# Two-layer trunk on one core: layer B's q as seven half-size block products, with a changed start and an fp32r broadcast

## The chip, the cores and the metric

The kernel runs on one core of a Trainium2 chip. The metric is the device time of one execution in microseconds. TensorE multiplies, VectorE and ScalarE work on the results in PSUM and SBUF, GpSimd (POOL) does a few element operations, SyncE (SP) and ScalarE issue the DMAs.

## The reference

Two layers over x of 1024 tokens by 1024 channels, batch 1, in fp32:

```python
# layer A (gMLP)
u, v, z = split(rms_norm(x) @ w_in)              # 1024 -> 3 x 2048
v = layer_norm(gelu(v))                          # then mixed along 128-token chunks, causal, 8 groups
h = x + rms_norm((gelu(u) * (w_s @ v + b_s) * silu(z)) @ w_out)
# shared keys and values
k, v = rms_norm(h) @ w_k, rms_norm(h) @ w_v      # 4 kv heads of 64
# layer B (sliding window of 128, attention sinks, ALiBi)
q, z = split(rms_norm(h) @ b_w_in)               # 16 heads of 64, and a gate of 1024
o = softmax(q k' / 8 + alibi, with a sink) @ v   # blocks of 128 tokens see the block before and their own
out = h + rms_norm((o * silu(z)) @ b_w_out)
```

## The kernel before, in words

Every product in fp32 is made of three fp32r matmuls: each operand is split into a high part (rounded to fp32r by a ScalarE copy) and a low part (the rest, a VectorE subtraction); mm3 (L168 to 171) adds hi x hi, hi x lo and lo x hi into one PSUM bank. A step of work on TensorE therefore needs splits on ScalarE and VectorE: split (L104 to 106), and split_scaled with a gain (L108 to 110).

The tokens are treated in two halves of 512 (half 0 and half 1), the channels in k-tiles of 128. Activations lie transposed, channels on partitions and 512 tokens on the free axis; a pair of tiles (pair) holds the high and low parts of all 8 k-tiles of one half.

The stages, in the order in which TensorE runs them, with the times of the profile:

- v, and then u and z of layer A, up to 490 us. These large products use a scheme of block products: the operands are cut in two along tokens, inner and outer dimension, and seven products of half-size blocks, of sums of blocks, replace eight. T[1] to T[7] are the seven sums of blocks on the activation side. uz_layer runs them in groups of four products (quads) with weight sums from POOL and VectorE. The row factors 1/rms of x are laid across the partitions in broadcast_rstd (L272 to 279): a diagonal matrix per half, multiplied by a matrix of ones in fp32 (L278), under the v products.
- The output product of layer A (out_layer), 490 to 654 us, in seven products too. Its tail, chain_a (L746 to 758), adds the residual for one half, stores h1, and takes the row factor r1 of the result. norm_h1 (L760 to 773) then multiplies by r1 (hb), transposes it on TensorE (nt), and splits it into n, the operand of layer B: n0 for half 0, n1 for half 1. For half 0 all this is done inside out_layer.
- Layer B in plain products. q of half 0 (654 to 701 us) runs with chain_a for half 1 as a side job, one side step per step of the main one. kv of half 0 (701 to 725 us) runs with norm_h1 of half 1 at its side, and z of half 0 (725 to 769 us) by itself.
- attn(0) (769 to 886 us) and attn(1) (894 to 1005 us): for each block of 128 tokens and half of the heads a unit of scores (s), masks and row maxima on VectorE, exponentials on ScalarE, transposes (pt), and products with v (o). TensorE alone would idle between them, so attn takes steps from a fill, a generator of other products: 64 steps in attn(0), which are kv, q and half of z for half 1; in attn(1) the rest of z and the first output products. The last output products end the kernel.

The weights of layer B come through the class Weights (L112 to 152): a written list, order, of transfers of 512 KB that are loaded into three raw buffers (wload) two places ahead and split one place ahead, in the order in which the products ask for them. Before, the list is q, kv and z for half 0, kv, q and z for half 1, then the output weights. A weight of q is so loaded and split twice, once for each half.

q_phase (L966 to 976) evacuates each of q's PSUM banks at once: a ScalarE copy with the head's scale (L971) for the high part, and a VectorE operation (L972) for the low part, both on 64 partitions for each parity of heads. kv_phase (L989 to 1020) ends with eight ScalarE copies of k (L1017, L1018), subtractions for k's low part (L1019) and copies of v. Unit (scores at L1050, exponentials at L1065) reads q, and kh and kl, the parts of k.

At the start (L403 to 427) SyncE's queue begins with x's first tile, and ScalarE's queue with the gains and then the first half of the first v weights. POOL makes the high part of those weights (L415), VectorE the low part (L418).

Rows of an engine stand in program order, and each engine takes its own rows in that order.

## Time and profile before

| | before |
|---|---|
| median of 3 runs | 1050.68 us (1050.01 to 1051.42) |
| the profiled execution | 1051.56 us |
| its span | 1049.8 us |
| mean granted TensorE clock | 0.998 |
| TensorE, busy share of the span | 99% |
| VectorE | 70% |
| ScalarE | 55% |
| POOL | 19% |

The profile is of one execution. Busy means that an instruction ran on the engine; matmuls overlap one another, so the rate of matmuls is read from the distance between the starts of two. A wait names the engine and line that waited, and the engine and line that ended the wait. In the chain of waits each piece of work is followed back to what released it. The windows of the trace give busy time and number of instructions for each engine in a stretch. In a row of groups the columns are: line, engine, operation, output and inputs with shapes, count, total us and mean ns, and the idle time ahead of them.

### The profile page before, as it was taken

The page shows a single profiled execution, that of the slowest core. Times are in us where ns is not written, and L with a number is a line of the kernel's source. Part 1 is how long each engine was busy: PE and PEld are TensorE (multiplying, and loading weights), DVE is VectorE, ACT ScalarE, POOL GpSimd, SP SyncE. Part 2 cuts the span into 40 slices and gives each one's busy share as a digit, 9 for nine tenths or more (in the row PEclk, how much of TensorE's full clock was granted, in tenths as well). Part 3 has the DMA queues.
Part 4 walks back from the last instruction along what each step waited for, and adds up shares of the span by engine and source line. Part 5 has one row for each costly group of instructions (what it writes and reads, how often), then busy time and mean ns, then how long its engine had stood idle before and what let it go on. Part 6 is the DMA issues. An engine that isn't in the chain of part 4 may idle for free.

```text
span 1049.8 us, 13661 instructions
## 1 busy us (share of the span) xinstructions
PE 1039.2 (99%) x4994; PEld 854.8 (81%) x4994; DVE 731.9 (70%) x1244; ACT 577.2 (55%) x989; POOL 195.2 (19%) x153
## 2 busy tenths in 40 slices
PE   9999999999999999999999999999999999999997
PEld 7888788888888888888888888888888777877776
DVE  6997466867768668677697587665247776667763
ACT  6683444555465565555444464654466665786631
POOL 0300003253342542530200000100001111011120
PEclk9999999999999999999999999999999999999999
DMA  8877252334333333347897642532222121211363
GB/s 310 271 282 269 101 177 88 116 105 143 124 121 116 132 124 117 108 137 272 322 352 270 201 160 93 200 102 86 95 81 71 51 81 61 81 61 61 121 220 120
DMA packets 80899, 157.56 MB, mean 150 GB/s; under 512 B 5824, under 2 KB 32704, under 8 KB 80832
## 3 DMA queue, kind: packets, MB, share of 16 engines
q1 hardware_dynamic: 76176, 147.75, 41.2%
q10 hardware_dynamic: 4656, 8.94, 2.4%
q8 instruction: 39, 0.64, 0.3%
q14 instruction: 28, 0.23, 0.1%
HBM read 125.21 MB, written 31.46 MB: 149 GB/s over the span
## 4 chain that ended last, share of the span: by engine, by line
PE 93%; DVE 4%; ACT 1%; issue 0%; DMA 0%; POOL 0%; DVEq 0%; POOLq 0%; ACTq 0%
PE ob L169 6%; PE ub L169 6%; PE ub L171 6%; PE ob L171 6%; PE ob L170 6%; PE ub L170 6%; PE qz L169 5%; PE qz L171 5%; PE qz L170 5%; PE uc L169 3%; PE uc L171 3%; PE uc L170 3%; PE s L1050 3%; PE sp L614 3%; PE vb L170 2%; PE vb L171 2%
## 5 line engine op out<-in xcount | busy, mean ns | idle before, releaser
L110 DVE SCALAR_TENSOR_TENSOR wlo<-raw_w,gn,whi 128x512 fp32r<-128x512 f32 x80 | 58.7, 758 | 62.2 <-ACT whi L109 62.0
L169 PE MATMUL qz<-n_hi,whi 128*128 128x512 f32 x256 | 101.0, 394 | 0.4 <-DVE q_lo L972 0.4
L171 PE MATMUL qz<-n_hi,wlo 128*128 128x512 f32 x256 | 100.0, 391 | 1.2 <-DVE wlo L110 1.2
L170 PE MATMUL qz<-n_lo,whi 128*128 128x512 f32 x256 | 99.8, 390 | 0.0
L109 ACT ACTIVATE whi<-raw_w,gn 128x512 fp32r<-128x512 f32 x80 | 54.9, 716 | 54.2 <-PE qz L170 35.0
L1065 ACT ACTIVATE pr<-pr,mx 128x129 f32<-128x129 f32 x128 | 50.0, 393 | 40.1 <-DVE mx L1061 40.0
L169 PEld LDWEIGHTS qz<-n_hi,whi 128*128 128x128 f32 x256 | 48.0, 188 | 16.6 <-issue 6.5
L105 ACT ACTIVATE uzhilo_g<-f 128x1024 fp32r<-128x1024 f32 x31 | 32.9, 1060 | 48.6 <-PE uc L171 42.7
L171 PEld LDWEIGHTS qz<-n_hi,wlo 128*128 128x128 f32 x256 | 48.0, 188 | 12.3 <-DVE wlo L110 2.1
L170 PEld LDWEIGHTS qz<-n_lo,whi 128*128 128x128 f32 x256 | 48.1, 188 | 9.3
L106 DVE TENSOR_TENSOR uzhilo_g<-f,uzhilo_g 128x1024 fp32r<-128x1024 f32 x31 | 39.0, 1257 | 19.9 <-ACT uzhilo_g L105 19.9
L209 ACT ACTIVATE uz_slots<-ub 128x512 f32<-128x512 f32 x48 | 28.3, 590 | 42.4 <-PE ub L171 39.0
L169 PE MATMUL ub<-T,whi_g 128*128 128x512 f32 x128 | 50.7, 396 | 0.0
L169 PE MATMUL ub<-T,uzhilo_g 128*128 128x512 f32 x128 | 50.5, 395 | 0.0
L171 PE MATMUL ub<-T,wlo_g 128*128 128x512 f32 x128 | 49.9, 390 | 0.0
L171 PE MATMUL ub<-T,uzhilo_g 128*128 128x512 f32 x128 | 49.9, 390 | 0.0
L170 PE MATMUL ub<-T,uzhilo_g 128*128 128x512 f32 x128 | 49.8, 389 | 0.0
L170 PE MATMUL ub<-T,whi_g 128*128 128x512 f32 x128 | 49.8, 389 | 0.0
L169 PE MATMUL uc<-T,uzhilo_g 128*128 128x512 f32 x124 | 48.9, 395 | 0.0
L170 PE MATMUL uc<-T,uzhilo_g 128*128 128x512 f32 x124 | 48.3, 389 | 0.0
L171 PE MATMUL uc<-T,uzhilo_g 128*128 128x512 f32 x124 | 48.3, 389 | 0.0
L105 ACT ACTIVATE whi_g<-raw_uz 128x1024 fp32r<-128x1024 f32 (+1 forms) x31 | 26.5, 854 | 36.7 <-PE ub L170 15.6
(332 smaller groups left out, 3071.4 us busy)
## 6 DMA issues: line engine op xcount, KB each, us to landing
raw_uz<-in_wuz_in_dram SPq DMA_DIRECT2D x32, 512.0 KB, 3.4
raw_w<-in_wqz_dram SPq DMA_DIRECT2D x32, 512.0 KB, 3.5
td<-uz_slots SPq DMA_DIRECT2D x56, 256.0 KB, 2.2
orawP2a<-td SPq DMA_DIRECT2D x28, 512.0 KB, 4.0
raw<-in_wv_in_dram SPq DMA_DIRECT2D x17, 512.0 KB, 4.8
vg<-vd SPq DMA_DIRECT2D x8, 1024.0 KB, 5.4
orawP2b<-in_wo_a_dram SPq DMA_DIRECT2D x16, 512.0 KB, 7.7
vraw<-in_wv_in_dram SPq DMA_DIRECT2D x13, 512.0 KB, 4.4
```

The source lines that it names most:

```text
L105: nc.scalar.activation(hi, src, AF.Copy)
L106: nc.vector.tensor_tensor(lo, src, hi.bitcast(F32), ALU.subtract)
L109: nc.scalar.activation(hi, src, AF.Copy, scale=g)
L110: nc.vector.scalar_tensor_tensor(lo, src, g, hi.bitcast(F32), ALU.mult, ALU.subtract)
L169: nc.tensor.matmul(out, lhsT=a_hi, rhs=b_hi, start=start, stop=False, skip_group_check=True)
L170: nc.tensor.matmul(out, lhsT=a_hi, rhs=b_lo, start=False, stop=False, skip_group_check=True)
L171: nc.tensor.matmul(out, lhsT=a_lo, rhs=b_hi, start=False, stop=stop, skip_group_check=True)
L209: nc.scalar.activation(out, a, AF.Copy)
L614: nc.tensor.matmul(psv[:, n], lhsT=d["vg"][:, 4 * j + n, i * P:(i + 1) * P], rhs=d["wc"], start=True, stop=True)
L1050: nc.tensor.matmul(pss[par][:, g, w0:256], lhsT=q[par][:, m, bs_], rhs=w[par][:, p, ks], start=g + k == 0, stop=g + k == 2, skip_group_che ...
L1065: nc.scalar.activation(pr[:, i], pr[:, i], AF.Exp, bias=mx[:, i:i + 1], scale=-1.0, accum_out=dn[:, i:i + 1])
```

## The change

Layer B's q, for both halves at once, becomes a stage of its own with seven block products. z of half 0 is put ahead of it, since the block sums need both halves' norms.

- norm_sums replaces norm_h1 for half 1: beside n1 it forms T[1] to T[7]. For each of the four token blocks VectorE makes three differences from the transposed bank (nt1) and splits of T5, T6 and T4, and POOL four additions; a last step splits T7. It runs as side job to z of half 0, after chain_a.
- q_tiles runs four quads of weights, each with seven products of 12 matmuls; its sums of weights are on POOL, its gains and splits on VectorE and ScalarE, its banks are copied or added into six slots and stored to DRAM (qd). The weights of q are loaded once.
- z of half 0 is stored to DRAM (zd) as it is made, and loaded back before attn(0), since its tiles serve as pieces for q_tiles.
- reload_q brings q back from qd, a transfer of 512 KB for each of four steps per half, and makes q's high and low parts with two ScalarE and two VectorE operations of 64 x 1024. Two steps for half 0 run under kv of half 0; the other two and the four of half 1 are a side job of attn(0).
- The tiles of attention (bp) are allocated, and their constants loaded, after q_tiles, not before. kv of half 0 follows q_tiles. attn(0) has a fill of 32 steps in place of 64, four of them taken ahead of the first scores.
- The list of weights is z, kv, kv, z, output weights, and stops after the first eight until q_tiles ends.
- broadcast_rstd multiplies in fp32r: the diagonal is split into two parts, four matmuls in all.
- At the start the first half of the first v weights leads SyncE's queue, and x's first tile goes to ScalarE's, behind the gains.

TensorE has 48 rows fewer. On VectorE, right behind the row factor of half 1 (r_1), the order in before is (yoa is h1 of half 1 by token block, wlo the low part of a weight, qz a bank of q, hb the normalised rows):

```order
L178 TENSOR_SCALAR r_1_90<-s_1_4999 128x4
L763 TENSOR_SCALAR hb_2_5318<-yoa_3_4273,r_1_90 128x1024
L110 SCALAR_TENSOR_TENSOR wlo_5097<-raw_w_5024,gn,whi_5096 128x4x128 x2
L972 SCALAR_TENSOR_TENSOR q_hi<-qz_0_0_4959,qsc,q_hi 64x512
L763 TENSOR_SCALAR hb_3_5352<-yoa_3_4273,r_1_90 128x1024
L972 SCALAR_TENSOR_TENSOR q_hi<-qz_0_1_4960,qsc,q_hi 64x512
L972 SCALAR_TENSOR_TENSOR q_lo<-qz_0_0_4959,qsc,q_lo 64x512
```

and in after (nt_2 is the transposed bank, t_2, qT and q_slots hold block sums):

```order
L180 TENSOR_SCALAR r_1_90<-s_1_5002 128x4
L786 TENSOR_SCALAR hb_2_5071<-yoa_3_4285,r_1_90 128x1024
L110 SCALAR_TENSOR_TENSOR wlo_5135<-raw_w_5027,gn,whi_5134 128x4x128 x2
L786 TENSOR_SCALAR hb_3_5149<-yoa_3_4285,r_1_90 128x1024
L106 TENSOR_TENSOR n_lo<-nt_2_0_5089,n_hi 128x4x128
L208 TENSOR_TENSOR t_2_5087<-nt_2_0_5089,n_hi 128x512
L106 TENSOR_TENSOR n_lo<-nt_2_1_5104,n_hi 128x4x128
L208 TENSOR_TENSOR q_slots<-nt_2_1_5104,n_hi 128x4x128
L208 TENSOR_TENSOR t_2_5088<-nt_2_1_5104,t_2_5087 128x512
```

The evacuations of q are gone from this place, and the sums and splits of the block operands stand there.

In attn(0), VectorE's order between the first units' scores in before (s are the scores, pr and mx probabilities and maxima, snk the sinks):

```order
L110 SCALAR_TENSOR_TENSOR wlo_5934<-raw_w_5805,gn,whi_5933 128x512
L1055 COPY_PREDICATED s_0_10_5911<-mrg,neg 128x2x128
L110 SCALAR_TENSOR_TENSOR wlo_5934<-raw_w_5805,gn,whi_5933 128x512
L1061 ISA pr_0_5839,mx_0_5840<-s_0_10_5911,bias,snk 128x128
L1061 ISA mx_0_5840 128x1
```

and in after (raw_q is the buffer of a reload):

```order
L1221 ISA pr_0_6199,mx_0_6200<-s_0_10_6255,bias,snk 128x128
L1221 ISA mx_0_6200 128x1
L1132 SCALAR_TENSOR_TENSOR q_hi<-raw_q_2_6249,qsc,q_hi 64x1024
L1132 SCALAR_TENSOR_TENSOR q_lo<-raw_q_2_6249,qsc,q_lo 64x1024
L1215 COPY_PREDICATED s_0_11_6256<-mrg,neg 128x2x128
L1221 ISA pr_0_6199,mx_0_6200<-s_0_11_6256,bias,snk 128x128
```

A weight's low half stood ahead of the scores s_0_10 and behind their mask; now a reload's two operations stand between s_0_10 and s_0_11.

The diff, cut to its core (what is left out is allocation and the code of functions named above that changes names only):

```diff
-            q, z = ([(wqz[i, m:m + 4, :, kq * 256:kq * 256 + 256].rearrange("m p c -> p m c"), f"q{kq}")
-                     for m in range(0, 8, 4) for kq in range(4)] for i in range(2))
+            z = [(wqz[1, m:m + 4, :, kq * 256:kq * 256 + 256].rearrange("m p c -> p m c"), f"q{kq}")
+                 for m in range(0, 8, 4) for kq in range(4)]
             kv = [(wkv[kp], f"kv{kp}") for kp in range(4)]
-            self.order += q + kv + z + kv + q + z
+            self.order += z + kv + kv + z
...
+            self.limit = 8
         def load(self, i):
-            while len(self.raw) <= min(i, len(self.order) - 1):
+            while len(self.raw) <= min(i, self.limit - 1):
...
+    def broadcast_rstd(pool):
+        ones_r = pool.tile([P, P], F32R, name="ones_r")
+        copy(ones_r, ones)
         for h in range(NH):
-            dg = sum_tile(f"dg{h}")[:, 0:512].rearrange("p (a b) -> p a b", a=4)
+            dg = st.tile([P, 2, 4, P], F32R, tag="xt", name=f"dg{h}")
             for j in range(4):
-                nc.vector.tensor_scalar(dg[:, j], ident, rx[h][:, j:j + 1], None, ALU.mult)
+                r = rx[h][:, j:j + 1]
+                nc.scalar.activation(dg[:, 0, j], ident, AF.Copy, scale=r)
+                nc.vector.scalar_tensor_tensor(dg[:, 1, j], ident, r, dg[:, 0, j].bitcast(F32),
+                                               ALU.mult, ALU.subtract)
             ps = bank("s", f"bc{h}")
-            nc.tensor.matmul(ps, lhsT=ones, rhs=dg.rearrange("p a b -> p (a b)"), start=True, stop=True)
+            for i in range(2):
+                nc.tensor.matmul(ps, lhsT=ones_r, rhs=dg[:, i].rearrange("p a b -> p (a b)"),
+                                 start=i == 0, stop=i == 1)
...
-        xload(xa[:, 0], 0, 0, 0, 1)
         r0 = raws.take("v0")
-        nc.scalar.dma_start(out=r0[:, 0:512], in_=wv_in[0, 0][:, 0:512])
+        load(r0[:, 0:512], wv_in[0, 0][:, 0:512])
+        xload(xa[:, 0], 0, 0, 0, 1, nc.scalar)
...
+        for t in (2, 3, 0, 1):
+            ts_ = slice(t * P, (t + 1) * P)
+            xt = st.tile([P, D], F32, tag="xt", name=f"hb1_{t}")
+            nc.vector.tensor_scalar(xt, yo[t], r1[1][:, t:t + 1], None, ALU.mult)
+            yield
+            t1, t2 = tmp("t1", t), tmp("t2", t)
...
+                split(n[0][:, ks, ts_], n[1][:, ks, ts_], ps)
+                if kq == 0:
+                    add(t1, ps, n_0[0][0][:, :, ts_].bitcast(F32), ALU.subtract)
+                    add(t1, t1, n_0[1][0][:, :, ts_].bitcast(F32), ALU.subtract, nc.gpsimd)
+                else:
+                    add(t3[:, :, ts_], ps, n[0][:, 0:HT, ts_].bitcast(F32), ALU.subtract)
+                    add(t2, ps, t1, ALU.subtract)
+                    add(t4, n_0[0][1][:, :, ts_].bitcast(F32), t2, ALU.subtract, nc.gpsimd)
+                    add(t3[:, :, ts_], t3[:, :, ts_], n[1][:, 0:HT, ts_].bitcast(F32), ALU.subtract, nc.gpsimd)
+                    add(t4, t4, n_0[1][1][:, :, ts_].bitcast(F32), ALU.add, nc.gpsimd)
+                yield
+            for m, src in ((6, t2), (5, t1)):
+                split(T[m][0][:, :, ts_], T[m][1][:, :, ts_], src)
+            yield
+            split(T[4][0][:, :, ts_], T[4][1][:, :, ts_], t4)
+            yield
+        T[7] = tuple(big.tile([P, HT, TH], F32R, tag=f"P1_{2 + i}", name=f"qT7_{i}") for i in range(2))
+        for i in range(2):
+            split(*(a[:, 2 * i:2 * i + 2] for a in T[7]), t3[:, 2 * i:2 * i + 2])
...
+        def product(q, m, ps, first):
+            hi, lo = ops[q][m]
+            for k in range(HT):
+                cs = slice(k * P, (k + 1) * P)
+                mm3(ps, hi[:, cs], lo[:, cs], T[m][0][:, k], T[m][1][:, k], first and k == 0, k == HT - 1)
...
+        def store(q, i, j, c):
+            nc.sync.dma_start(out=qd[j][q][:, i], in_=c)
...
+        for q in range(5):
+            live = q < 4
+            if live:
+                b = bank("mm", f"qb{q}")
+                product(q, 1, b, True)
+                c00 = slot()
+                copy(c00, b)
+            else:
+                weights.limit = len(weights.order)
+                weights.load(weights.at + 1)
+            if q > 0:
+                pb, pcc, c01 = prev
+                product(q - 1, 4, pb, False)
+                c10 = slot()
+                copy(c10, pb)
+                store(q - 1, 1, 0, c10)
+            if live:
+                a = bank("s", f"qa{q}")
+                product(q, 2, a, True)
+                add(c00, c00, a, ALU.add)
+                store(q, 0, 0, c00)
+                prep1(q + 1)
+            else:
+                weights.split(weights.at)
+            if q > 0:
+                product(q - 1, 3, pcc, False)
+                add(c01, c01, pcc, ALU.add)
+                store(q - 1, 0, 1, c01)
+                del ops[q - 1]
+            if not live:
+                break
+            prep3(q)
+            product(q, 6, b, False)
+            c01 = slot()
+            copy(c01, b)
+            cc = bank("mm", f"qc{q}")
+            product(q, 5, cc, True)
+            prep2(q + 1)
+            fetch(q + 2)
+            product(q, 7, b, False)
+            c11 = slot()
+            copy(c11, b)
+            add(c11, c11, cc, ALU.add)
+            store(q, 1, 1, c11)
+            prev = (b, cc, c01)
...
+    def reload_q(h, q):
+        for i in range(4):
+            r = raw_tile(f"q{h}_{i}").rearrange("p (m t) -> p m t", m=2)
+            nc.sync.dma_start(out=r, in_=qd[h][i])
+            ms = slice(2 * i, 2 * i + 2)
             for par in range(2):
                 rw, ot = half[par], half[1 - par]
-                g = qsc[rw, m // 4:m // 4 + 1]
-                nc.scalar.activation(q[par][rw, m], ps[rw], AF.Copy, scale=g)
-                nc.vector.scalar_tensor_tensor(q[par][ot, m], ps[rw], g, q[par][rw, m].bitcast(F32),
+                g = qsc[rw, i // 2:i // 2 + 1]
+                nc.scalar.activation(q[par][rw, ms], r[rw], AF.Copy, scale=g)
+                nc.vector.scalar_tensor_tensor(q[par][ot, ms], r[rw], g, q[par][rw, ms].bitcast(F32),
                                                ALU.mult, ALU.subtract)
-        for m in range(0, 8, 4):
-            yield from qz_four(h, 0, m, n, evac)
-    def z_phase(h, n, z, m0, m1):
+            yield
...
+                if keep:
+                    nc.sync.dma_start(out=zd[m // 2], in_=zs)
...
+    def attn(h, q, z, fill, total, late=0, first=0, side=iter(())):
         taken = [0, 0]
+        for _ in range(first):
+            step(fill)
...
+            step(side)
...
+    side = chain(chain_a(1, yo, ss), norm_sums(n1, yo, n0))
+    z0 = [qp.tile([P, 4, TH], F32, tag=f"half{i}", name=f"z0_{i}") for i in range(2)]
+    main = z_phase(0, n0, z0, 0, 8, keep=True)
+    qs = q_tiles()
     step(main, main)
-    for _ in main:
+    for i, _ in enumerate(main):
         step(side)
+        if i in (22, 27):
+            step(qs)
...
+    drain(qs)
+    qp_ctx.close()
...
+    side = chain(reload_q(0, q0))
+    z0 = [big.tile([P, 4, TH], F32, tag=f"P1_{2 * i}", name=f"z0_{i}") for i in range(2)]
+    for i, _ in enumerate(kv_phase(0, n0)):
+        if i in (1, 6):
+            step(side)
+    for i in range(4):
+        nc.sync.dma_start(out=z0[i // 2][:, i % 2 * 2:i % 2 * 2 + 2], in_=zd[i])
+    z1 = [big.tile([P, 4, TH], F32, tag=f"P1_{2 * i}", name=f"z1_{i}") for i in range(2)]
     q1 = pair("P3", "q1")
-    fill = chain(kv_phase(1, n1), q_phase(1, n1, q1), z_phase(1, n1, z1, 0, 4))
-    attn(0, q0, z0, fill, 64)
+    fill = chain(kv_phase(1, n1), z_phase(1, n1, z1, 0, 4))
+    attn(0, q0, z0, fill, 32, first=4, side=chain(side, reload_q(1, q1)))
```

More of the change, by code (lines that the diff above doesn't have):

```diff
@@ L984, in evac @@
                 nc.scalar.activation(zs, zs, AF.Silu)
+                if keep:
+                    nc.sync.dma_start(out=zd[m // 2], in_=zs)
         for m in range(m0, m1, 4):
[L987 removed]
+            yield from z_four(h, m, n, evac)
     def kv_phase(h, n):
[L990 to L991 removed]
+        pk = [bank("mm" if h else "s", f"pk{h}_{i}") for i in range(2)]
+        pv = [bank("mm" if h else "s", f"pv{h}_{i}") for i in range(2)]
         for kp in range(4):
@@ L1104, in values @@
             split(q[0][:, ms, bs_], q[1][:, ms, bs_], yt)
-    def attn(h, q, z, fill, total, late=0):
+    def attn(h, q, z, fill, total, late=0, first=0, side=iter(())):
         taken = [0, 0]
+        for _ in range(first):
+            step(fill)
         n = 34 if late else 40
@@ L1218, in tile_yoco @@
-    drain(side)
-    drain(z_phase(0, n0, z0, 0, 8))
+    drain(qs)
+    qp_ctx.close()
+    bp = ctx.enter_context(tc.tile_pool(name="bp", bufs=1))
+    bias = bp.tile([P, 4, P], F32, name="bias")
+    nc.sync.dma_start(out=bias.rearrange("p a b -> p (a b)"), in_=consts[:, C_BIAS:C_BIAS + 512])
+    mrg = bp.tile([P, P], F32, name="mrg")
+    nc.sync.dma_start(out=mrg, in_=consts[:, C_MERGE:C_MERGE + P])
+    neg = bp.tile([P, 1], F32, name="neg")
+    nc.vector.memset(neg, -1e30)
+    kh = [bp.tile([P, 2, S], F32R, name=f"kh{i}") for i in range(2)]
```

131 lines of the change are left out of this document (94 added, 37 removed).

## The prediction

> **What bounds the kernel now.** I read the page first, then TensorE's waits, then the rates of single instructions, and last the busy times by stage. The page's span and its chain by engine:
>
> ```profile
> span 1049.8 us, 13661 instructions
> ...
> PE 93%; DVE 4%; ACT 1%; issue 0%; DMA 0%; POOL 0%; DVEq 0%; POOLq 0%; ACTq 0%
> ```
>
> TensorE carries the chain. Everything it waited for, outside the last stage's idle end (columns: engine and line, what it waited for, us in total, times, longest):
>
> ```profile
> PE qz L171 <- DVE wlo L110: 1.2, 2, 0.7
> PE warm L924 <- DVE small L93: 1.1, 1, 1.1
> PE vb L169 <- POOL whi_v L415: 0.5, 1, 0.5
> PE qz L169 <- DVE q_lo L972: 0.4, 1, 0.4
> PE vb L169 <- ACT ve L209: 0.3, 1, 0.3
> PE vb L170 <- DVE wlo_v L418: 0.2, 1, 0.2
> ```
>
> Under 4 us in all: a matmul less is time less, as long as nothing else comes late. So the question is what the removed matmuls uncover. The profiled execution took 1051.56 us, 1.8 more than its span and 0.88 above the median of the runs, 1050.68. I sum changes against 1051.56 and take 0.88 off at the end. About 0.2% (2.1 us) is what a measurement of this kernel can tell from no change.
>
> **Matmuls removed.** Two neighbours in the timeline (start, duration), and the old broadcast in the chain (start, length):
>
> ```profile
> 655.00 0.39 PE L170 MATMUL qz<-n_lo,whi 128*128 128x512 f32 x1
> 655.68 0.39 PE L170 MATMUL qz<-n_lo,whi 128*128 128x512 f32 x1
> 106.08 1.72 PE bc L278 x4
> ```
>
> Three matmuls start in 0.68 us: 0.227 each, though each is listed with 0.39. Layer B's q took 8 products by 8 k-tiles by 3 matmuls for each half, 384; now 4 quads x 7 products x 12 = 336. 48 x 0.227 = **-10.9**. The broadcast becomes four fp32r matmuls at 0.23: 1.72 - 0.9 = **-0.8**. Its diagonals move to ScalarE and VectorE under the v matmuls, and TensorE had no wait there.
>
> **Start.** The first matmuls wait for weights, not for x:
>
> ```profile
> 5.78 1.24 POOL L415 CAST whi_v<-raw_v 128x512 fp32r<-128x512 f32 x2 [5.28 <-DMA raw_v<-in_wv_in_dram]
> 6.45 0.98 PE L169 MATMUL vb<-whi_v,T 128*128 128x512 f32 x3 [0.51 <-POOL whi_v L415]
> 7.63 0.51 PE L170 MATMUL vb<-wlo_v,T 128*128 128x512 f32 x1 [0.20 <-DVE wlo_v L418]
> ```
>
> The weight transfer moves from second on ScalarE's queue to first on SyncE's. The idle times in the brackets, 0.5 and 0.2, are the most there is to win; x comes later in turn, so I take **-0.3** (-1 to +0.5).
>
> **Waits of before that go.** The two qz rows of the waits sit in q(0), where weight splits and q's evacuations shared VectorE: 1.2 + 0.4 = **-1.6** (if the splits still come late, -0.4). The four together: -13.6.
>
> **Stage z(0): T operands must be made.** The new order runs z(0) first, and under it all seven block operands are built from both halves' norms. Half 1's norm needs r1:
>
> ```profile
> 654.10 0.39 PE L169 MATMUL qz<-n_hi,whi 128*128 128x512 f32 x1
> 672.36 1.01 POOL L179 TENSOR_TENSOR r<-r,small 128x4 f32<-128x4 f32 x1 [12.68 <-DVE r L178]
> 673.40 0.76 DVE L763 TENSOR_SCALAR hb<-yoa,r 128x1024 f32<-128x1024 f32 x1 [1.12 <-POOL r L179]
> 674.07 1.41 DVE L110 SCALAR_TENSOR_TENSOR wlo<-raw_w,gn,whi 128x512 fp32r<-128x512 f32 x2
> 707.60 1.28 DVE L106 TENSOR_TENSOR n_lo<-nt,n_hi 128x512 fp32r<-128x512 f32 x2
> 23.35 1.22 DVE L206 TENSOR_TENSOR sch<-vraw,raw 128x1024 f32<-128x1024 f32 x1
> 702.41 0.87 PE nt L769 x8
> ```
>
> After r1 before's VectorE had four hb, eight n_lo splits, weight halves and q's evacuations to do, spread over q(0) and kv(0), 71 us; now all of it, with 24 more sums and splits for the operands, stands in one queue under z(0)'s 48 us (both queues' beginnings stand in the section on the change). Counted from TensorE's first matmul of the stage (654.1): r1 is there at 673.4, 19.3 us in. Behind it VectorE does hb 4 x 0.75 = 3.0, weight halves 8 x 0.705 = 5.6, 20 operations on a PSUM bank at 0.64 = 12.8, 12 between SBUF tiles at 0.6 (half of the 1.22 row) = 7.2, the two halves of T7 2.4, the first scaled q weight 1.2 and its split 1.2: 33.4, so q's first low half is ready at 52.7. TensorE has 192 matmuls of z and 4 of q at 0.227 (44.5) and four groups of transposes at 0.87 (3.5): it is there at 48.0. **+4.7**. Bounds: 2.3 if only the wait for hb_2 shows (TensorE reaches its transposes 17.7 us in, after 78 matmuls, and hb_2 is there at 20.0), 11 if ScalarE's high halves and POOL's 16 additions put one third of that queue's 20 us of sums on top.
>
> The four quads behind it I cost at nothing: per quad VectorE has two scalings and three splits of 1.2, one half split and three additions of 0.64, 8.6 us under 84 x 0.227 = 19.1 us of matmuls. Should that cover go, each 1 us too late in a quad costs 4. The stores of q and z are not waited for until the reloads, a stage later.
>
> **Entry of attn(0).** The first scores need half 0's k, and only one step pair of kv(1) stands between them and kv(0)'s last matmul, where before all of z(0) did:
>
> ```profile
> L1017 ACT ACTIVATE kh<-pk 64x512 fp32r<-64x512 f32 x4 | 2.4, 593 | 2.2 <-PE pk L171 2.2
> 704.50 0.28 PE L169 MATMUL pv<-whi,n_hi 128*128 128x256 f32 x1
> 704.62 0.28 PE L170 MATMUL pv<-wlo,n_hi 128*128 128x256 f32 x1
> ```
>
> Six ScalarE copies at 0.59 and one subtraction at 0.64 are 4.2; the pair covers 6 x 0.227 + 12 x 0.12 = 2.8: **+1.4** (0 to 3).
>
> **attn(0).** Its fill loses 16 steps of q for the reloads. The stage, and three stretches with busier engines (columns: window, length; then busy us and instructions of TensorE, its weight loads, VectorE, ScalarE, POOL; clock, DMA share, GB/s):
>
> ```profile
> 769.00:886.40 117.40, 116.95 (x646) 92.85 (x644) 87.83 (x250) 76.34 (x208) 15.29 (x14) 1.00 0.20 64
> 20.00:50.00 30.00, 30.00 (x133) 24.49 (x132) 29.99 (x31) 17.32 (x22) 8.22 (x2) 1.00 0.78 264
> 826.00:851.00 25.00, 24.55 (x128) 18.93 (x127) 21.14 (x62) 17.15 (x50) 3.28 (x3) 1.00 0.20 64
> 800.00:890.00 90.00, 89.56 (x450) 67.76 (x449) 68.04 (x184) 56.63 (x152) 14.19 (x13) 1.00 0.20 65
> ```
>
> TensorE had 116.95. Between the first scores and the last values stand 254 qz matmuls in before and 127 of z in after, 24 of pv and 12 of pk less: 116.95 - 127 x 0.227 - 24 x 0.12 - 12 x 0.227 = 82.5. What moved out is paid elsewhere and in the 48. VectorE's rows:
>
> ```profile
> L110 DVE SCALAR_TENSOR_TENSOR wlo<-raw_w,gn,whi 128x512 fp32r<-128x512 f32 x33 | 24.6, 772 | 13.9 <-ACT whi L109 13.9
> L972 DVE SCALAR_TENSOR_TENSOR q_lo<-qz,qsc,q_lo 64x512 fp32r<-64x512 f32 x8 | 6.0, 755 | 1.2 <-ACT q_lo L971 1.0
> 659.71 2.48 DVE L753 SCALAR_TENSOR_TENSOR yoa<-yoa,rpa,xa 128x1024 f32<-128x1024 f32 x2 [1.19 <-POOL rpa L179]
> ```
>
> From 87.83 go 16 evacuations (two groups of 8 like the q_lo row, 12.0) and 16 weight halves (11.3 at 0.705); 12 reload operations of 1,024 columns at 1.24 come (14.9): 79.4. TensorE and VectorE now need almost the same time, so VectorE's own gaps decide. The stretch from 20 to 50 us says what happens where nothing else binds it (30.0 of 30 busy, TensorE without a gap: stall 0), that from 826 to 851 runs at 0.85 (79.4 / 0.85 = 93.4, stall 10.9). In attn(0) itself VectorE's gaps were
>
> ```profile
> DVE dn L1070 <- ACT pr L1065: 4.4, 5, 0.9
> DVE z L1103 <- PE o L1099: 1.7, 1, 1.7
> DVE q_lo L106 <- ACT q_hi L105: 1.4, 2, 0.7
> ```
>
> waits inside a unit's own chain of scores, exponentials and values, which stay: 7.5 of the 90 us window. At a density of 1 - 7.5/90 = 0.917 the stage takes 86.6, **+4.1** over TensorE's 82.5 (0 to 10.9). The others of its waits were for weights or transposes that stood behind q's matmuls and go with them.
>
> **Sum**: -13.6 + 4.7 + 1.4 + 4.1 = **-3.4**: 1048.2 for the profiled execution, **1047.3** as a median. The matmuls' gain is real, and three quarters of it is handed back to VectorE. With the bounds of the three stalls, 2.3 to 11, 0 to 3 and 0 to 10.9, its own range is about 1040 to 1053; all three at one end at once is unlikely, so 1042.5 to 1052.
>
> **Rivals.**
>
> **A, slower: the reloads stop VectorE's queue.** Six reload steps lie in attn(0), each a transfer of 512 KB, then ScalarE's high half and VectorE's low half. VectorE takes its instructions in order, and in after the reload's two stand between one unit's scores, so their lateness delays what TensorE waits for:
>
> ```profile
> raw_w<-in_wqz_dram SPq DMA_DIRECT2D x32, 512.0 KB, 3.5
> ```
>
> A transfer of this size lands 3.5 us after its issue, and ScalarE's copy of 1,024 columns adds some 1.1 (twice the kh row's 0.59, less the fixed part): 4.6 us from a free buffer to VectorE's turn. If a quarter of that is uncovered at each step, 1.15 x 6 = 6.9 come on top of the forecast: **1054.2**. It decides from 3.4 / 6 = 0.6 us lost at each step. For it: the two operations stand ahead of the same unit's next scores. Against it: three raw buffers let a transfer start early, and the DMA engines are only 0.20 busy in the stage.
>
> **B, all but the norm hidden.** VectorE is as dense as at 20 to 50 us, and the entry's copies are done beneath kv(1): -13.6 + 4.7 = -8.9, **1041.8**. For it: the dense stretch, and the idle VectorE of the waits was mostly slack. Against it: units depend on ScalarE at each step.
>
> **C, no change: POOL and VectorE hold each other up.** In the first layer POOL's addition of two tiles next to a busy VectorE ran longer than undisturbed ones:
>
> ```profile
> L206 POOL TENSOR_TENSOR f<-raw_uz,f 128x512 f32<-128x512 f32 x15 | 22.4, 1495 | 0.0
> L206 POOL TENSOR_TENSOR f<-raw_uz,raw_uz 128x512 f32<-128x512 f32 x15 | 19.2, 1281 | 127.2 <-DVE uzhilo_g L106 127.2
> ```
>
> 0.2 us each. If VectorE loses that at each of the 16 additions that POOL does in z(0), its queue there is 3.4 longer and TensorE waits for all of it: -3.4 + 3.4 = 0.0, **1050.7**. The Trainium skill states this as a rule ("SBUF — State Buffer", section "Who interferes with whom"): a VectorE operation with both inputs in SBUF and a GpSimd operation that reads SBUF share a port pair, and the one that comes second is blocked for the whole of the other. An estimate by that rule alone, with a whole 1.28 us lost at each of the 16, would be 20.5 us more. The 0.2 of the trace bears out that there is a cost, and not one of that size.
>
> That the change doesn't do what it says is excluded by the order: 48 rows less on TensorE.
>
> **How the numbers follow.** The forecast 0.43, B 0.22, A 0.22, C 0.13. B and most of the forecast's own range (0.33 of 0.43) are faster by over 0.2%, 0.55; C and 0.08 of the forecast lie within 0.2%, with 0.02 of C's on the slow side, 0.19; A, that and 0.02 of the forecast are slower, 0.26. The range reaches down past B to 1040.5 (B with the bound of 2.3 in z(0) would be 1039.4), and up past A to 1056.5 (a third of the 4.6 uncovered at each step: 1.53 x 6 = 9.2); I leave about 0.1 out on either side.
>
> **What would show it.** In the profile of after: TensorE waits at the first transposes and at qb for a low half, 4 to 5 us in the z(0) and q stages together; s of the first unit waits 1 to 2 us for kl or kh; between the first s and the last o of half 0 the stage is near 86.6 us with VectorE over 0.9 busy. Waits of q_hi or q_lo on the reload's ScalarE copy or on its transfer, over 0.6 us each, would speak for A; a stage of 83 us for B; POOL additions over 1.4 us in z(0) with TensorE waiting longer there for C. The forecast is wrong if the q stage itself shows waits, since I gave it none.

## The result and the profile after

The changed kernel takes 1077.18 us (median of 4 runs, 1076.08 to 1078.50) against 1050.78: a ratio of 1.0247, interval 1.0235 to 1.0260. The prediction was 1047.3 within 1040.5 to 1056.5. The profiled execution has a span of 1076.2 us. One execution of the last kernel below ran at a clock of 0.75 for 1300.5 us and is not counted. The busy times on the page of before, and then the page of the changed kernel, its first lines, its granted clock by slice and its chain by engine:

```profile
PE 1039.2 (99%) x4994; PEld 854.8 (81%) x4994; DVE 731.9 (70%) x1244; ACT 577.2 (55%) x989; POOL 195.2 (19%) x153
```

```profile
span 1076.2 us, 13702 instructions
...
PE 1042.0 (97%) x4946; PEld 851.3 (79%) x4946; DVE 768.8 (71%) x1258; ACT 589.8 (55%) x998; POOL 249.0 (23%) x185
...
PEclk9999999999999999999999999889999979999999
...
PE 83%; DVE 8%; ACT 3%; POOL 2%; issue 2%; DMA 1%; POOLq 0%; DVEq 0%; ACTq 0%
```

TensorE has 48 matmuls less and yet is busy for longer, 1042.0 against 1039.2: some of them ran slowly. The mean granted clock is 0.984 in place of 0.998. With it the 26.4 us more of the span come apart into three parts:

| us | before | after | change |
|---|---|---|---|
| TensorE's work at the full clock (busy x clock) | 1037.1 | 1025.3 | -11.8 |
| busy time lost to a lower clock | 2.1 | 16.7 | +14.6 |
| idle (span less busy) | 10.6 | 34.2 | +23.6 |

The clock is given to three digits, so the first two rows hold to about half a us. The saving came in full, and over three times as much was lost. TensorE's longest waits in the changed kernel say where (columns as before):

```profile
PE qb L171 <- ACT whi_q L105: 5.4, 1, 5.4
PE z L173 <- DVE wlo L110: 4.5, 2, 3.3
PE o L1257 <- POOL pc L1243: 4.2, 3, 1.9
PE pt L1238 <- DVE pr L1231: 3.6, 2, 2.2
PE s L1210 <- ACT pc L1239: 2.6, 2, 1.7
PE qc L171 <- ACT qhilo_q L105: 1.7, 1, 1.7
PE nt L794 <- DVE hb L786: 1.4, 1, 1.4
```

qz's waits are gone. nt, z, qb and qc stand under z(0) and in the first quad of q; o, pt and s stand in attn(0). By stage (z's first matmul to q's first, to the first scores, to half 0's last values; busy us of TensorE, its weight loads, VectorE, ScalarE, POOL, then the clock):

```profile
655.10:718.00 62.90, 51.35 (x225) 40.75 (x223) 51.86 (x64) 32.94 (x58) 25.86 (x18) 0.92 0.35 126
718.00:826.40 108.40, 106.70 (x516) 89.80 (x517) 52.57 (x62) 43.05 (x59) 28.23 (x18) 0.98 0.44 144
826.40:927.90 101.50, 90.65 (x485) 67.66 (x483) 84.81 (x235) 78.12 (x199) 17.04 (x14) 0.92 0.24 78
```

At the full clock TensorE's work in them is 47.2, 104.6 and 83.4; lost are 15.7, 3.8 and 18.1 (the clock's two digits leave 0.3 to 0.5 open in each). Layer B also begins 1.0 us later (655.1 against 654.1).

### The profile page after: what moved, and what is told of

Read it like the earlier page. It is cut to its first block, busy times and chain, and to the rows that moved or that the text cites. A ratio compares the mean times of both kernels' runs of the same rounds, so it can differ in the third digit from the quotient of the medians.

```text
span 1076.2 us, 13702 instructions
## 1 busy us (share of the span) xinstructions
PE 1042.0 (97%) x4946; PEld 851.3 (79%) x4946; DVE 768.8 (71%) x1258; ACT 589.8 (55%) x998; POOL 249.0 (23%) x185
## 4 chain that ended last, share of the span: by engine, by line
PE 83%; DVE 8%; ACT 3%; POOL 2%; issue 2%; DMA 1%; POOLq 0%; DVEq 0%; ACTq 0%
PE ob L171 6%; PE ub L171 5%; PE ub L173 5%; PE ob L173 5%; PE ob L172 5%; PE ub L172 5%; PE uc L171 3%; PE uc L173 3%; PE uc L172 3%; PE sp L623 3%; PE vb L171 2%; PE vb L173 2%; PE vb L172 2%; PE oc L173 2%; PE oc L172 2%
## 5 line engine op out<-in xcount | busy, mean ns | idle before, releaser
L173 PE MATMUL z<-n_hi,wlo 128*128 128x512 f32 x128 | 51.9, 405 | 4.6 <-DVE wlo L110 4.5
L171 PE MATMUL z<-n_hi,whi 128*128 128x512 f32 x128 | 52.6, 411 | 0.2 <-ACT z L1139 0.2
L172 PE MATMUL z<-n_lo,whi 128*128 128x512 f32 x128 | 51.4, 401 | 0.0
L208 POOL TENSOR_TENSOR f<-raw_uz 128x512 f32<-128x512 f32 x15 | 20.1, 1339 | 127.1 <-DMA raw_uz<-in_wuz_in_dram 85.0
L171 PE MATMUL uc<-T,uzhilo_g 128*128 128x512 f32 x124 | 48.9, 395 | 0.0
L208 POOL TENSOR_TENSOR f<-raw_uz,raw_uz 128x512 f32<-128x512 f32 x15 | 19.2, 1282 | 127.3 <-DVE uzhilo_g L106 127.3
L1242 POOL TENSOR_SCALAR_AFFINE_SELECT pp<-pc 128x1024 f32<-128x1024 f32 x14 | 16.0, 1144 | 131.2 <-ACT pc L1239 131.2
L105 ACT ACTIVATE whi_g<-raw_uz 128x1024 fp32r<-128x1024 f32 (+1 forms) x31 | 26.5, 855 | 35.8 <-PE ub L172 13.6
L110 DVE SCALAR_TENSOR_TENSOR wlo<-raw_w,gn,whi 128x512 fp32r<-128x512 f32 x48 | 38.6, 833 | 10.2 <-ACT whi L109 10.0
L109 ACT ACTIVATE whi<-raw_w,gn 128x512 fp32r<-128x512 f32 x48 | 32.8, 715 | 23.1 <-PE oc L173 7.6
```

The costliest lines, as they stand in the source:

```text
L105: nc.scalar.activation(hi, src, AF.Copy)
L109: nc.scalar.activation(hi, src, AF.Copy, scale=g)
L110: nc.vector.scalar_tensor_tensor(lo, src, g, hi.bitcast(F32), ALU.mult, ALU.subtract)
L171: nc.tensor.matmul(out, lhsT=a_hi, rhs=b_hi, start=start, stop=False, skip_group_check=True)
L172: nc.tensor.matmul(out, lhsT=a_hi, rhs=b_lo, start=False, stop=False, skip_group_check=True)
L173: nc.tensor.matmul(out, lhsT=a_lo, rhs=b_hi, start=False, stop=stop, skip_group_check=True)
```

## The experiments

The theory after this result: under z(0) the sums for the block operands cost the loss, and in attn(0) the reloads of q do. Rivals: VectorE's own load there (the prediction's reason), the thin fill in attn(0), and the granted clock. A loss below is a stage's length less TensorE's work in it at the full clock. Two expectations take attn(0) over a slightly shorter stretch (94.2 and 100.1 us) and so have other losses for it.

**The two small edits, each alone on the kernel before.**

```diff
+        load(r0[:, 0:512], wv_in[0, 0][:, 0:512])
+        xload(xa[:, 0], 0, 0, 0, 1, nc.scalar)
```

> The kernel before with only the changed start: v's first half weights lead SyncE's queue, x's first tile goes behind the gains on ScalarE's. In the profile of the changed kernel the v products start 0.6 us later (40.6 against 40.0), and x's first tile is what the first high half waits for (5.85 against 4.23). If the start edit causes this, this kernel is 0.6 us slower than before (1051.4); if the shift comes from the broadcast's new preparations, which share ScalarE and VectorE there, it is as fast as before or 0.3 faster.

1051.96 against 1051.40, ratio 1.0006 (0.9997 to 1.0015): not told from nothing. In its own profile the first matmul starts at 6.17 us, earlier than before's 6.45; in the changed kernel's it starts at 6.72:

```profile
5.85 1.34 ACT L423 ACTIVATE T<-xa,gn 128x512 fp32r<-128x512 f32 x2 [2.44 <-DMA xa<-in_xT_dram]
...
6.72 0.47 PE L171 MATMUL vb<-whi_v,T 128*128 128x512 f32 x1 [0.96 <-ACT T L423]
```

The weights' cast now starts at 4.1, but x's first tile lands so late that T follows at 5.85, and the first matmul waits for x. The same holds at 6.17: with this start x's tile comes last, and when it lands differs between the two profiles.

```diff
-            nc.tensor.matmul(ps, lhsT=ones, rhs=dg.rearrange("p a b -> p (a b)"), start=True, stop=True)
+            for i in range(2):
+                nc.tensor.matmul(ps, lhsT=ones_r, rhs=dg[:, i].rearrange("p a b -> p (a b)"),
+                                 start=i == 0, stop=i == 1)
```

> The kernel before with only the broadcast in fp32r. By the prediction's price, 1.72 - 0.9 us, it is 0.8 faster (1049.9). The changed kernel reached the u and z products 0.9 us late, 0.3 more than the v products at 40 us: if the broadcast's preparations hold TensorE up, it is 0 to 0.5 slower instead.

1051.10 against 1051.40, ratio 0.9998 (0.9990 to 1.0007): no more than the 0.8 that was expected, and not told from nothing. Neither edit explains the result. The 1.0 us by which layer B begins later arise by 55 us, where vb waits for ScalarE's ve: it goes on at 53.4 in the profile of before, at 54.4 in those of both small edits, and at 54.8 in the changed kernel's. ve waits there for a row factor from POOL, which stands behind POOL's work on wc; whether the edits move that is open.

**z(0): all sums left out.** Only half 1's norm is made; the products use blocks of n0 and n1.

```diff
-        T[4] = tuple(big.tile([P, HT, TH], F32R, tag=f"P1_{i}", name=f"qT4_{i}") for i in range(2))
+        T[4] = tuple(t[:, 0:HT] for t in n)
+        T[5], T[6], T[7] = T[1], T[2], T[3]
...
-                if kq == 0:
-                    add(t1, ps, n_0[0][0][:, :, ts_].bitcast(F32), ALU.subtract)
```

> The changed kernel with only half 1's norm under z(0): the sums and splits for T4 to T7, 24 VectorE operations, 16 POOL additions and 16 ScalarE copies, are left out, and the products take the blocks of n0 and n1 that lie there anyway. What is left on VectorE behind r1 is 4 x 0.75 + 8 x 0.72 + 8 x 0.64 + 2.4 = 16.3. If those sums are what z(0) loses, the stage from z's first matmul to q's first goes from 62.9 to about 48.5, and the whole to 1061 to 1063. If it is the transposes' wait for r1 and the weight splits behind it, it stays over 53.

1064.89 (ratio 1.0129, 1.0113 to 1.0144), and its stage under z(0):

```profile
654.60:703.50 48.90, 47.42 (x226) 39.13 (x224) 31.19 (x42) 26.42 (x45) 9.73 (x7) 1.00 0.52 184
```

48.9 in place of 62.9, at the full clock. The sums cost 14.0 there and 12.3 of the whole.

**z(0): POOL's additions moved to VectorE.**

```diff
-                    add(t1, t1, n_0[1][0][:, :, ts_].bitcast(F32), ALU.subtract, nc.gpsimd)
+                    add(t1, t1, n_0[1][0][:, :, ts_].bitcast(F32), ALU.subtract)
```

> The changed kernel with norm_sums' 16 POOL additions on VectorE. Theory 1 (collisions): in z(0) POOL's additions and VectorE's operations on two SBUF tiles block each other (VectorE's splits there took 1.1 to 1.8 in place of 0.6, POOL's additions up to 2.1 in place of 1.28) and ScalarE waits for POOL between them; without POOL the stage from z's first matmul to q's first, 62.9 us, becomes 54 to 58, and the whole 1069 to 1073. Theory 2 (VectorE's own load): 16 additions of 0.6 more on the full queue make the stage 9.6 longer, 72, and the whole 1086.

1075.85 (1.0238, 1.0224 to 1.0252): neither number. The stage is 61.4 us long:

```profile
655.00:716.40 61.40, 49.46 (x226) 40.09 (x224) 53.36 (x82) 35.91 (x61) 2.02 (x2) 0.94 0.41 147
```

The same instruction, the split of T6 and T5, first in the changed kernel and then here (mean ns behind the total):

```profile
L106 DVE TENSOR_TENSOR qT<-t,qT 128x512 fp32r<-128x512 f32 x8 | 11.0, 1376 | 1.1 <-ACT qT L105 1.1
```

```profile
L106 DVE TENSOR_TENSOR qT<-t,qT 128x512 fp32r<-128x512 f32 x8 | 5.5, 688 | 1.3 <-ACT qT L105 1.3
```

Beside POOL it takes twice as long. A split with one input in PSUM doesn't, in the changed kernel (one of the eight starts at 680.57, while POOL adds from 680.06 to 681.79):

```profile
L106 DVE TENSOR_TENSOR n_lo<-nt,n_hi 128x512 fp32r<-128x512 f32 x8 | 5.5, 681 | 1.2 <-ACT n_hi L105 1.2
```

Without POOL the doubling goes, but 16 additions of 0.68 come on VectorE: the collisions and the load were both right, and nearly cancel.

**z(0): the same additions left out.** T4, T5 and T7 hold unfinished sums.

```diff
-                    add(t1, t1, n_0[1][0][:, :, ts_].bitcast(F32), ALU.subtract, nc.gpsimd)
...
-            split(T[4][0][:, :, ts_], T[4][1][:, :, ts_], t4)
+            split(T[4][0][:, :, ts_], T[4][1][:, :, ts_], t2)
```

> The changed kernel without norm_sums' 16 additions: they are left out, not moved, so T4, T5 and T7 hold unfinished sums, and VectorE's queue under z(0) is the one that the prediction counted, 33.4 us behind r1 (with two more scalings of 1.2 ahead of q's first low half in this order: 35.8). If that count was right and only POOL's part was missed, the stage from z's first matmul to q's first is 52 to 55 us (62.9 in the changed kernel). If VectorE stands still for ScalarE between its short operations without POOL too, it stays over 57.

1065.62 (1.0131, 1.0114 to 1.0147), the stage:

```profile
654.70:706.00 51.30, 47.57 (x225) 39.00 (x223) 43.54 (x66) 34.49 (x61) 2.01 (x2) 1.00 0.46 160
```

51.3, a little under the expectation: with all of VectorE's counted work TensorE loses 3.7. VectorE takes 34.8 us from its first hb (673.5) to the end of q's first low half (708.3), and 35.8 were counted. The 16 additions on POOL, with the waits for their results, cost the other 11.6. In the changed kernel VectorE's operations on two SBUF tiles are some 9 us longer in sum than here, and ScalarE waits 14.0 us for POOL's sums. On VectorE the 16 additions, begun 0.6 apart, are 9.6, which on 51.3 make 60.9, near the 61.4.

**The clock: the gap ahead of q filled.** 22 matmuls whose result isn't read.

```diff
+        for i in range(22):
+            nc.tensor.matmul(dummy, lhsT=T[1][0][:, 0, 0:P], rhs=T[1][0][:, 0], start=i == 0, stop=i == 21,
+                             skip_group_check=True)
```

> The changed kernel with 22 idle matmuls (4.99 us at 0.227) in the gap of 5.4 us ahead of q's first product; their result isn't read. In the changed kernel the matmuls behind that gap start 0.43 apart for 4 us, in place of 0.227, with the granted clock at 0.84. If the gap itself lowers the clock, the matmuls behind it now start 0.227 apart, and the whole is 1.9 us shorter (1075.3). If the clock was low for another reason, nothing changes or it gets longer by up to 5.

1081.10 (1.0283, 1.0267 to 1.0298): the whole got 3.9 longer, against the expectation, but the place itself did what was expected. The changed kernel, behind its gap of 5.36 us, and up to where the full rate returns:

```profile
718.01 0.79 PE L171 MATMUL qb<-n_hi,whi_q 128*128 128x512 f32 x1 [5.36 <-ACT whi_q L105]
...
719.02 0.63 PE L171 MATMUL qa<-n_hi,whi_q 128*128 128x512 f32 x1
719.45 0.63 PE L172 MATMUL qa<-n_lo,whi_q 128*128 128x512 f32 x1
...
722.22 0.39 PE L173 MATMUL qb<-n_hi,wlo_q 128*128 128x512 f32 x1
722.45 0.39 PE L171 MATMUL qb<-n_hi,whi_q 128*128 128x512 f32 x1
```

and with the gap filled:

```profile
718.86 0.50 PE L171 MATMUL qb<-n_hi,whi_q 128*128 128x512 f32 x1 [0.43 <-ACT whi_q L105]
...
720.70 0.40 PE L172 MATMUL qb<-n_lo,whi_q 128*128 128x512 f32 x1
720.93 0.39 PE L173 MATMUL qb<-n_hi,wlo_q 128*128 128x512 f32 x1
```

Starts are 0.43 apart for 4.0 us behind the gap; without it they are 0.34 apart right behind a short wait and otherwise 0.23. So the gap lowers the clock. The time was given back in the next wait, for the copy that frees q's bank:

```profile
PE qb L171 <- ACT q_slots L211: 4.5, 1, 4.5
```

That wait isn't in the changed kernel. There ScalarE makes this copy (727.11) ahead of its second split of qhilo_q (728.10); with the idle matmuls, which take a bank, the copy (729.29) stands behind that split (728.33), which waits for POOL's sum. So the order changed too, and the whole says nothing on the clock.

**attn(0): the thin fill alone, on the kernel before.** q of half 1 is put ahead of attn(0), which keeps 32 steps; the list of weights is put in the same order (not shown).

```diff
+    drain(q_phase(1, n1, q1))
+    fill = chain(kv_phase(1, n1), z_phase(1, n1, z1, 0, 4))
+    attn(0, q0, z0, fill, 32)
```

> The kernel before with q of half 1 ahead of attn(0), so that attn(0) has the changed kernel's fill, 32 steps of kv and z of half 1, and nothing else of the change: no reloads, no stores, no block products. The same matmuls. If the thin fill is what costs attn(0) its 10 us, this kernel is 8 to 11 us slower than before (1059 to 1062). If the reloads and VectorE's load are the cause, it is as fast as before or 2 us slower (1051 to 1053).

1056.63 (1.0055, 1.0040 to 1.0070), between the two. attn(0) is 84.1 us long, its TensorE busy 79.93 at the full clock:

```profile
812.30:896.40 84.10, 79.93 (x479) 61.84 (x477) 70.44 (x225) 59.67 (x184) 15.66 (x14) 1.00 0.16 51
```

It loses 4.2: thinning the fill is a part, not the bulk.

**attn(0): more fill.** The eight steps come out of attn(1), which takes 44 in place of 48 (not shown).

```diff
-    attn(0, q0, z0, fill, 32, first=4, side=chain(side, reload_q(1, q1)))
+    attn(0, q0, z0, fill, 40, first=4, side=chain(side, reload_q(1, q1)))
```

> The changed kernel with 40 fill steps in attn(0) in place of 32: eight of the z steps of half 1 that attn(1) had. If attn(0) stalls because its fill is too thin to cover a unit's chain of scores, exponentials, transposes and selections, attn(0)'s idle time falls by about 4 of its 11 us, and the whole to 1073 or 1074 as long as attn(1) still covers itself with 40. If VectorE's load is the bound there, the time stays (1077), since eight more steps bring eight more weight halves.

1084.43 (1.0309, 1.0292 to 1.0326): wrong both ways. attn(0) kept its length (101.4) with eight z steps more in it, so its loss did fall, to 12.7 (101.4 less 90.50 at a clock of 0.98); attn(1), which lost them, then stalled, and from half 0's last values to the end it takes 153.8 (1083.2 - 929.4) in place of 148.3.

**attn(0): half 1's q by transfers alone.** Its scale and split are left out.

```diff
+                nc.sync.dma_start(out=q[par][:, 2 * i:2 * i + 2].bitcast(F32), in_=qd[h][i])
```

> The changed kernel with half 1's q put into both its tiles by transfers alone: the scale and the split of half 1's q, eight ScalarE operations of 1.15 and eight VectorE operations of 1.28 in attn(0), are left out. If the reloads' engine work and its place in the queues cost the most of attn(0)'s excess (94.2 us against 82.5 of matmuls), the stage falls to 86 or less and the whole to about 1069. If attn(0) is held up by the thin fill and by k's copies of half 1 in the middle of the units instead, the stage stays over 91 and the whole over 1074.

1075.58 (1.0222, 1.0204 to 1.0239), attn(0) 95.8 in place of 101.5: between the two.

```profile
826.20:922.00 95.80, 85.97 (x468) 64.75 (x469) 72.33 (x225) 64.69 (x187) 16.03 (x14) 0.95 0.26 91
```

Two reload steps of half 0 still stood in it, so the next kernels move those.

**attn(0): half 0's reloads early; then half 1's late, or by transfers alone; and no steps ahead.**

```diff
-        if i in (1, 6):
+        if i in (1, 6, 10, 14):
             step(side)
```

> The changed kernel with all four reload steps of half 0's q under kv of half 0; only half 1's four stay in attn(0). attn(0) loses 18.9 us in the changed kernel (100.1 us long against 81.2 of matmuls at the full clock); the thin fill alone lost 4.2 and half 1's reloads some 4.7. If the two reload steps at its beginning bring the rest (the first one makes VectorE wait 1.9 us between the first unit's scores), it loses 10 to 12 here, and the whole is 1069 to 1071. If not, it stays at 17 to 19 and 1077.

1079.91 (1.0277, 1.0261 to 1.0292): no gain. Only one of the two steps left the stage, though: VectorE's part of the fourth runs from 829.9 to 832.5, and attn(0) begins at 825.7. With half 1's steps in the stage, moving that one out brings nothing (100.8 in place of 101.5; attn(0) is 99.6 and 101.2 in two kernels that don't touch it).

```diff
-    attn(0, q0, z0, fill, 32, first=4, side=chain(side, reload_q(1, q1)))
+    attn(0, q0, z0, fill, 32, first=4)
     drain(fill)
+    drain(reload_q(1, q1))
```

> As the kernel with early reloads of half 0, and half 1's four reload steps behind attn(0), so that attn(0) has none. If reloads explain all beyond the thin fill, attn(0) now loses 4 to 6 us; the four steps then stand open between the two attentions at up to 2.3 us each, so the whole says little, 1068 to 1076. If attn(0) still loses over 10, it is the place of k and v of half 1 in the fill.

1073.76 (1.0216, 1.0199 to 1.0233); its profiled execution, with a span of 1067.7, is the shortest of four. attn(0) has none of half 1's steps left, and one of half 0's.

> The kernel with half 0's reloads early, and half 1's q put into its tiles by transfers alone (scale and split left out). attn(0) was 100.8 us with half 1's full reloads and 89.1 with none. If the ScalarE and VectorE operations of the reloads cost the 11.7, it is 88 to 91 here; if the transfers do (they hold up the weights on SyncE's queue, or land late), it stays over 96.

1068.68 (1.0167, 1.0152 to 1.0182); again scale and split of half 1's q are left out. attn(0) with early reloads of half 0, and half 1's full, late, and by transfers alone:

```profile
825.70:926.50 100.80, 88.52 (x471) 66.85 (x469) 82.27 (x233) 72.38 (x195) 17.28 (x14) 0.90 0.23 74
```

```profile
825.10:914.20 89.10, 82.08 (x470) 63.31 (x469) 73.49 (x227) 66.68 (x190) 16.62 (x14) 0.98 0.19 60
```

```profile
826.00:915.20 89.20, 81.74 (x471) 63.21 (x469) 71.90 (x226) 63.72 (x187) 15.98 (x14) 0.98 0.28 95
```

100.8, 89.1, 89.2. The transfers cost nothing; the 16 ScalarE and VectorE operations of half 1's reloads cost 11.6, part of it by the clock (0.90 against 0.98). They take 10.4 of VectorE (82.27 - 71.90). That is their cost with three of half 0's steps ahead of the stage. In the changed kernel, with two of them in it, leaving half 1's out brought only 5.7 (101.5 to 95.8): VectorE then waits 4.69 us for the first of those two. Half 1's operations and the place of that step together cost 12.3 (101.5 to 89.2), and the runs don't divide that between them.

```diff
-    attn(0, q0, z0, fill, 32, first=4, side=chain(side, reload_q(1, q1)))
+    attn(0, q0, z0, fill, 32, first=0, side=chain(side, reload_q(1, q1)))
```

> The changed kernel with no fill step ahead of attn(0)'s first scores, so that all 32 lie within it, as in the kernel with the thin fill. If the four steps that were taken ahead are missed inside, attn(0) loses 3 to 5 us less, and the first scores wait 2 to 4 us for k: 1075 to 1077. If the place of half 1's k and v copies within the first units is what hurts, they move on by four steps and attn(0) loses as much or more: 1077 to 1081.

1072.71 (1.0209, 1.0193 to 1.0225), 2.3 faster than the lower end. attn(0) is 94.3 with as many matmuls, in the longest of the four executions (1075.82, the others 1072.0 to 1072.7):

```profile
824.20:918.50 94.30, 83.71 (x484) 63.59 (x484) 84.80 (x236) 74.49 (x197) 17.18 (x14) 0.98 0.27 84
```

It loses 12.3 in place of 18.1; the first scores wait 0.9 for k. The fill that was taken ahead had been missed inside.

**All that helped, together.**

```diff
-    attn(0, q0, z0, fill, 32, first=4, side=chain(side, reload_q(1, q1)))
+    attn(0, q0, z0, fill, 32)
     drain(fill)
+    drain(reload_q(1, q1))
```

> The changed kernel with the edits that helped, together: norm_sums' additions on VectorE, half 0's reloads all under its kv, half 1's behind attn(0), and no fill step ahead of the first scores. The single gains were 1.3, 3.4 and 4.5 us; added up 1068. Below 1064 the edits help one another (fewer gaps, a clock that stays up); over 1072 they fix the same loss twice. None of it makes up for the sums under z(0), so it stays slower than before.

1067.61, ratio 1.0157 (1.0140 to 1.0174): the gains add up (1068 was their sum), and no version beats the kernel before. attn(0) is as short as with the thin fill alone:

```profile
820.90:904.80 83.90, 79.25 (x474) 60.78 (x474) 72.86 (x228) 64.14 (x187) 16.64 (x14) 1.00 0.21 68
```

The sums under z(0) are left, and the reloads stand open between the attentions.

## Why the prediction was wrong

**Right**: the matmuls. -10.9 and -0.8 were forecast, and TensorE's work fell by 11.8. Its work under z(0) was to be 48.0, and is 47.2; in attn(0) 82.5, and is 83.4.

**Start, -0.3**: not measurable (+0.6, interval -0.3 to +1.6); the first matmul starts 0.3 earlier in the small edit's profile and 0.3 later in the changed kernel's. The step read the two waits for weights as the whole limit; x's tile, one place later behind the gains, became the last to come.

**The waits that go, -1.6**: those rows went, but waits for weight splits came back as 4.5 us on z.

**z(0), +4.7**: 15.7. The count of VectorE's 33.4 us held (34.8 measured, where two more scalings make the count 35.8): without POOL's additions the loss is 3.7. The step that failed is leaving POOL out of the forecast; even the upper bound of 11, which gave it a share, was too low. Rival C had the mechanism, a wait between POOL and VectorE, but priced it at 0.2 for each of 16 additions from rows of a stage where VectorE had room: 3.4. It costs 11.6. The Trainium skill's rule ("SBUF — State Buffer", section "Who interferes with whom"), that the second of two such operations is blocked for the whole of the first, gave an estimate of 20.5; the trace agrees with its direction and a little over half its size, and speaks against the 3.4. VectorE's splits between SBUF tiles doubled from 0.69 to 1.38, and ScalarE's splits and VectorE's behind them waited for POOL in turn.

**The quads of q, 0**: 3.8, in the first quad alone: 1.7 of waiting for qc's operand and the low clock behind the gap.

**Entry, +1.4**: nothing. The first scores don't wait for k; with no steps ahead they wait 0.9.

**attn(0), +4.1**: 18.1. VectorE's work was put at 79.4 and is 84.8. Of the 5.4 more, 4.5 are weight halves: 19 stand in the stretch in place of before's 30, so 11 went and not 16, and one takes 0.857 on the mean in place of 0.774. VectorE's density, put at 0.917, is 84.8 / 101.5 = 0.84, that of the stretch at 0.85 which gave the upper bound. The failed step is to take only the waits inside a unit's chain as lasting. The thin fill alone loses 4.2. That this is what was forecast for all is chance: the forecast had it from VectorE's load. The four steps of fill taken ahead, which the prediction counted only as cover for k, cost 4 to 6 more: 12.3 is lost without them in place of 18.1, and 4.6 (83.9 - 79.25) in place of 8.7 (89.1 less 82.08 at 0.98) where half 1's reloads are out too. Half 1's reload operations cost 5.7 to 11.6, by what else stands in the stage, though VectorE was not full. Rival A had their place right, in VectorE's and ScalarE's queues between the operations of the units, and 6.9 for it. Its reason is the smaller part. The first reload in attn(0) of the changed kernel, on ScalarE and VectorE:

```profile
832.87 1.15 ACT L1131 ACTIVATE q_hi<-raw_q,qsc 64x1024 fp32r<-64x1024 f32 x1 [1.26 <-DMA raw_q<-qd]
```

```profile
834.06 1.28 DVE L1132 SCALAR_TENSOR_TENSOR q_hi<-raw_q,qsc,q_hi 64x1024 fp32r<-64x1024 f32 x1 [1.93 <-ACT q_hi L1131]
```

Here the transfer is late, and VectorE stands still for 1.93 us between two scores of one unit, as A said. But over the stage such waits of VectorE are 3.4 in all, and half 1's steps cost nothing when only the transfers were left: it is the operations that cost, 2.3 us on ScalarE and 2.6 on VectorE at each step. That they do it by putting off the units' scores and exponentials is the likely reading; no run shows it by itself.

**The clock**: not in the prediction. 14.6 of the 26.4 us are busy time at a lower clock, some 13.5 of it in the three stretches shown above. So each us of a long gap cost more than a us. Rivals A and C together, with their prices of 6.9 and 3.4 on the forecast, make 1057.6, still 20 us short. Taking the rivals one at a time, where two of them and the clock came together, is the last step that failed.

**The range**: its working doesn't add up. The three upper bounds (11, 3 and 10.9) on -13.6 make 1062.0, not the 1053 given as the end of the range; and 1062.0 is still 15 us short.

What stays open: how the reloads' 11.6 us divide between ScalarE and VectorE, which were only taken away together, and between the two halves' steps, whose costs don't add up.

## What to carry to other kernels

When a tuned kernel's matmuls are traded for sums, splits and reloads, the sum has to be made for the stage where those stand: here 11.8 us of TensorE were saved over the whole, and 34 lost in two stages, though VectorE and ScalarE were 30 and 45% free on the page. An addition moved to POOL isn't free beside a VectorE that reads two SBUF tiles: here it cost about as much as a VectorE operation. Price a gap on TensorE by its length and by the slow matmuls behind it.

## What the runs showed of the hardware

Behind a gap of 5.4 us TensorE's matmuls started 0.43 apart for 4.0 us and then 0.23 again; with the gap filled, 0.23 but for 0.34 right behind a short wait. The Trainium skill ("TensorE: Matmul & The Clock Gate", section "HAM oscillation — how this bites in real kernels") puts the limit at about 3.4 us of idling, and halves the rate. The halved rate agrees; the limit doesn't hold here for a single gap, since in attn(0), where no wait is over 2.2 us, it came behind one of 2.16:

```profile
840.40 1.06 PE L1238 MATMUL pt<-ident,pr 128*128 128x128 f32 x8 [2.16 <-DVE pr L1231]
...
842.88 0.63 PE L173 MATMUL pk<-n_hi,wlo 128*128 128x512 f32 x1
843.31 0.63 PE L171 MATMUL pk<-n_hi,whi 128*128 128x512 f32 x1
```

Here too starts are 0.43 apart, and 0.23 ahead of the gap.

A VectorE split of 128x512 between SBUF tiles took 1.38 us on the mean beside POOL's additions and 0.69 without; one with an input in PSUM took 0.68 beside them too. Those additions took 1.5 in place of 1.28:

```profile
L208 POOL TENSOR_TENSOR q_slots<-q_slots,n_lo 128x512 f32<-128x512 f32 x8 | 12.1, 1515 | 4.7 <-DVE q_slots L208 4.3
```
